# One guard-row tile for two stages, and Toeplitz blocks fetched beside the sample heads

## Chip, cores and metric

The kernel runs on one core of one Trainium2 chip. The metric is the device time of one execution in microseconds (us). Three executions of the kernel before took 2793.55, 2795.27 and 2795.65 us; the median is 2795.27 us.

## What is computed

One layer of a hybrid streaming trunk, in float32, for 2048 prompt frames and 64 frames of a running stream with a 2048-frame cache:

```python
def _layer(x, lp, past):
    h = _rms(x, lp['ln1'])
    q, k, v, fg, u, hc, gb, gc = jnp.split(h @ lp['w_in'], SPLITS, axis=-1)
    ...                                            # q, k normed per head; logf = log_sigmoid(fg + bf)
    att = _fox_prompt(q, k, v, logf)               # 8 heads of 64; or _fox_sample with the caches
    y_ssm, hr, hi = _s5(u, ...)                    # diagonal state space, 16 groups of 16 channels, 64 states
    g = jax.nn.gelu(y_ssm)
    ssm = g * jax.nn.sigmoid(g @ lp['w_glu'] + lp['b_glu'])
    conv, conv_state = _short_conv(hc, gb, gc, lp['conv_w'], conv_prev)
    x = x + concat([_rms(att), _rms(ssm), _rms(conv)]) @ lp['w_out']
    f = jax.nn.relu(_rms(x, lp['ln2']) @ lp['w_up'])
    return x + (f * f) @ lp['w_down'], ...
```

In the attention, a score is `q.k/8 + c_q - c_k`, with c the running sum of the log forget gates, masked causally. The softmax is taken over all earlier frames.

## The kernel before

The stages run one after another: `phase1` (norm, in-projection, convolution; until about 543 us), the attention over eight heads (until about 1200 us), the out-projection, and the two matrices of the feed-forward part. The change touches the end of `phase1` and the attention.

**Scores and guard rows.** A head's transposed scores are two matmuls into a PSUM tile `st`: L1239 with `kb` (67 rows) against `q1`, L1240 with `ka` against `q2`. Rows 0 to 63 of `q1` are the query's high part, rows 64 and 65 are ones (against the forget-gate sums of `kb`, which come from `nc_d`), and row 66 is the guard: minus the row's maximum score, so that the exponential stays in range. `row_max` (L1131) computes that guard. For each of 16 query tiles it multiplies `q1` with `kb` into tiles `mx` (L1149), reduces each into `pm` on the DVE (L1154), transposes the result (`mxt`), copies it to `mt` (L1163) and sends it out by DMA (L1164).

While head h runs, the maxima of head h+1 are computed a piece at a time (`max_items`), and L1164 writes row 66 of the next `q1` from the SP queue. Head 0 has no head before it. Its maxima are computed inside `phase1` (`head0`, L488), where `q1` does not exist yet. So L1164 sends them from ACT's queue to row 2 of the DRAM tensor `m_d`, whose rows 0 and 1 were filled with ones at the start (L557), and L1207, on ACT's queue too, reads all three rows back into `q1`.

**Loads.** `load(h+1)` (L1200 to L1204) issues on the SP queue, at the first unit of head h, the five transfers of the next head's `kb`, `q1` and `ka`. `load_q2` (L1220, L1221) fetches 512 columns of `q2` in two halves, `load_v` (L1212) the 1 MB of `v`. All tile names are per buffer, and two heads' sets alternate. SP issues its DMAs in program order; an instruction that has to wait holds up all behind it. A scheduler has placed the instructions on their queues; the order of emission is that of the code.

**The filler chain.** Between the attention's units, `fill(w)` draws work from one generator, `chain()`: first most of the S5 branch (`s5_branch`), then the 64 sample queries' attention over the cache for head pairs 0 and 1, then pairs 2 and 3 (`sample_attention`), then the rest of the S5 branch and the preparation of the out-projection (`w_out_tiles`, which loads `wo_u` in four transfers). A `yield y` with y over 0 means that the chain pauses for y on a clock that advances with the units; each step drawn also costs a budget. `side_by_side` runs two such generators each with its own clock.

In `s5_branch`, L921 to L924 fetch the Toeplitz matrix `s5mt` from the DRAM tensor `kp_d`: eight transfers of 256 KB on the SP queue, with a `yield 1` after each. After them POOL computes the state recurrence (L931 to L935), and later sends out the final states (L952, L953). `s5mt` is first used after the sample attention.

Of the kernel before, what the change touches and what calls it, by code (L numbers as in the profile page):

```python
# [9 lines left out]
F32 = mybir.dt.float32  # L10
F32R = mybir.dt.float32r
# [8 lines left out]
NP = 2048  # L20
# [28 lines left out]
def f32(ap):  # L49
    return ap.bitcast(F32)  # L50
# [6 lines left out]
def setup(ctx, tc, I, O):  # L57
    g = Ctx()
    nc = tc.nc
    g.tc, g.nc, g.I, g.O = tc, nc, I, O  # L60
    g.dram = ctx.enter_context(tc.tile_pool(name="dram", bufs=1, space=DRAM))
    g.const = ctx.enter_context(tc.tile_pool(name="const", bufs=1, reuse_waits="tile"))
    dram, const = g.dram, g.const

    g.qk_d = [dram.tile([2, 2, 128, NP], F32, name=f"qk_d{i}") for i in range(4)]
    g.v_d = [dram.tile([2, 128, 16, 2 * HD], F32, name=f"v_d{i}") for i in range(4)]
    g.u_d = dram.tile([NT, CH], F32, name="u_d")
    g.mix_d = dram.tile([D, NT], F32, name="mix_d")
    g.kp_d = dram.tile([16, 16, 368], F32, name="kp_d")
    g.r_d = [dram.tile([H, 512], F32, name=f"r_d{i}") for i in range(4)]  # L70
    g.x2_d = dram.tile([NT, D], F32, name="x2_d")
    g.h_d = dram.tile([D, NT], F32, name="h_d")
    g.f_d = dram.tile([DFF, NT], F32, name="f_d")
    g.m_d = dram.tile([3, NP], F32, name="m_d")
    g.l_d = dram.tile([H, NP], F32, name="l_d")
    g.nc_d = dram.tile([3, H, NP], F32, name="nc_d")
    g.s5_d = dram.tile([128, S5N + 256], F32, name="s5_d")
    g.ncs_d = dram.tile([2, H, PAST + NS], F32, name="ncs_d")

    warm = const.tile([128, 1], F32, name="warm")  # L80
    nc.vector.memset(warm, 1.0)
    nc.scalar.activation(warm, warm, AF.Sqrt)
    g.ones = const.tile([128, 1], F32, name="one")
    nc.vector.memset(g.ones, 1.0)
    g.ident = const.tile([128, 128], F32, name="ident")
    make_identity(nc, g.ident)
    g.identb = const.tile([128, 128], BF16, name="identb")
    nc.vector.tensor_copy(g.identb, g.ident)
    g.maskq = const.tile([128, 256], BF16, name="maskq")
    nc.gpsimd.memset(g.maskq, 0.0)  # L90
    nc.gpsimd.affine_select(out=g.maskq, in_=g.maskq, pattern=[[-1, 256]], compare_op=ALU.is_ge,
                            fill=NEG, base=0, channel_multiplier=1)
    g.maskk = const.tile([128, 256], BF16, name="maskk")
    nc.gpsimd.memset(g.maskk, 0.0)
    nc.gpsimd.affine_select(out=g.maskk, in_=g.maskk, pattern=[[1, 256]], compare_op=ALU.is_ge,
                            fill=NEG, base=-128, channel_multiplier=-1)

    g.qbd = const.tile([128, 4, 128], F32, name="qbd")
    nc.vector.memset(g.qbd, 0.0)
    g.kts = const.tile([128, 4, NS], F32, name="kts")  # L100
    g.vs_d = dram.tile([NS, ATT], F32, name="vs_d")
    return g

# [64 lines left out]
def phase1(ctx, g):  # L168
    tc, nc, I, O = g.tc, g.nc, g.I, g.O
    dram = g.dram  # L170
# [8 lines left out]
    sp = ctx.enter_context(tc.tile_pool(name="p1s", bufs=4, reuse_waits="tile"))  # L179
    ps = ctx.enter_context(tc.tile_pool(name="p1ps", bufs=1, reuse_waits="tile", space=PSUM))  # L180
# [283 lines left out]
    for b in range(3):  # L464
# [4 lines left out]
        for gi in range(2):  # L469
            for ti in range(len(BLOCKS[b][gi][1])):  # L470
# [3 lines left out]
                elif gi == 0:  # L474
                    i = where[b - 1, 1 + ti, 0]
                    at(i - 1, loader_x(b, gi, ti))
                    at(i, prepper(b, gi, ti, i))
                else:
                    i = where[b, 0, 0] + ti - 1
# [8 lines left out]
    def head0():  # L488

        r = slice(0, 64)  # L490
        g.mxb = 2
        kt = xtp.tile([128, 8, 384], F32R, tag="xh0", name="kb_h0").rearrange("p k n -> p (k n)")
        qt = xtp.tile([128, 8, 384], F32R, tag="xl0", name="q1_h0").rearrange("p k n -> p (k n)")
        nc.sync.dma_start(f32(kt)[0:64, :NP], g.qk_d[0][0, 1, r, :])
        nc.sync.dma_start(f32(kt)[64:66, :NP], g.nc_d[0:2, 0, :])
        nc.gpsimd.memset(f32(qt)[64:66, :NP], 1.0)
        nc.sync.dma_start(f32(qt)[0:64, :NP], g.qk_d[0][0, 0, r, :])
        yield
        yield from row_max(g, sp, ps, qt, kt, 0, g.m_d[2:3])

    def s5_start():
        sc = xtp.tile([128, 8, 384], F32, tag="xl0", name="s5p").rearrange("p k n -> p (k n)")
# [5 lines left out]
    for i, (b, ci, gi, ti) in enumerate(work):  # L508
# [26 lines left out]
        if len(tails) > 3:  # L535
            f = tails.pop(0)
# [10 lines left out]
def gate_consts(ctx, g):  # L547
    nc, I = g.nc, g.I
    gp = ctx.enter_context(g.tc.tile_pool(name="gate", bufs=1, reuse_waits="tile"))
    tri = gp.tile([128, 128], F32, name="tri")  # L550
    nc.gpsimd.memset(tri, 1.0)
    nc.gpsimd.affine_select(out=tri, in_=tri, pattern=[[1, 128]], compare_op=ALU.is_ge,
                            fill=0.0, base=0, channel_multiplier=-1)
    ones = gp.tile([128, 128], F32, name="ones")
    nc.gpsimd.memset(ones, 1.0)
    nc.gpsimd.dma_start(g.nc_d[2].rearrange("h (a b) -> (h a) b", b=128), ones)
    nc.gpsimd.dma_start(g.m_d[0:2].rearrange("h (a b) -> (h a) b", b=128), ones[0:32])  # L557
    cl = gp.tile([128, 17, H], F32, name="cl")
    nc.vector.memset(cl[64:128, 16, :], 0.0)
    nc.sync.dma_start(cl[:, 0:16, :], I["cache_logf"][0, 0].rearrange("(t p) h -> p t h", p=128))  # L560
    return gp, tri, ones, cl
# [224 lines left out]
def s5_branch(g, pool, sp):  # L786

    nc, I, O = g.nc, g.I, g.O
# [129 lines left out]
        nc.sync.dma_start(hs[hh, 129, :], I[src][0, 0].rearrange("g p -> p g"))  # L918

    mt = pool.tile([128, G, 256], F32, tag="gm", name="s5mt")  # L920
    for t in range(8):  # L921
        nc.sync.dma_start(mt[16 * t:16 * t + 16],
                          g.kp_d[:, :, 16 * (7 - t):16 * (7 - t) + 256].rearrange("g c n -> c g n"))
        yield 1  # L924
    r1 = sp.tile([128, 16, G], F32, tag="yg", bufs=3, name="s5r1")
    r2 = sp.tile([128, 16, G], F32, tag="yg", bufs=3, name="s5r2")

# [200 lines left out]
        yield 0  # L1128


def row_max(g, sp, ps, q1, kb, h, dst):  # L1131

    nc = g.nc
    pm = sp.tile([128, 16, 4], F32, tag="pm", bufs=1, name=f"pm{h}")
    nc.vector.memset(pm, -3e38)
    for t in range(16):
        left, k0, cuts = t + 1, 0, []
        while left:
            w = min(left, 4)
            if left == 5:  # L1140
                w = 3
            cuts.append((k0, w))
            k0 += w
            left -= w
        for c, (k0, w) in enumerate(cuts):
            p = ps.tile([128, 512], F32, tag="mx", bufs=g.mxb, name=f"mx{h}_{t}_{c}")
            last = c == len(cuts) - 1
            n = max(w * 128, 256)
            nc.tensor.matmul(p[:, :n], q1[0:66, t * 128:t * 128 + 128], kb[0:66, k0 * 128:k0 * 128 + n], start=True,  # L1149
                             stop=not last)  # L1150
            if last:
                m = 256 if t == 0 else 128
                nc.tensor.matmul(p[:, n - m:n], g.identb, g.maskq[:, :m], start=False, stop=True)  # L1153
            nc.vector.tensor_reduce(pm[:, t, c:c + 1], p[:, :n], axis=AX.X, op=ALU.max)  # L1154
            yield
    nm = sp.tile([128, 16], F32, tag="nm", bufs=1, name=f"nm{h}")
    nc.vector.tensor_reduce(nm, pm, axis=AX.X, op=ALU.max, negate=True)
    yield
    yield
    pt = ps.tile([128, 512], F32, tag="mx", bufs=g.mxb, name=f"mxt{h}")  # L1160
    nc.tensor.transpose(pt[:16, :128], nm, g.ident)
    mt = sp.tile([16, 128], F32R, tag="mt", bufs=1, name=f"mt{h}")
    nc.vector.tensor_copy(mt, pt[:16, :128])  # L1163
    (nc.sync if h else nc.scalar).dma_start(f32(dst), f32(mt))  # L1164
    yield


def attention(ctx, g, fill):
# [14 lines left out]
    for i in range(2):  # L1183
# [9 lines left out]
            nc.gpsimd.memset(f32(q1[i])[64:67, :], 1.0)  # L1193
        nc.gpsimd.memset(f32(v3[i])[:, :, 128:130], 1.0)

    def load(h):
        i, hp, e = h % 2, h // 2, h % 2
        r = slice(64 * e, 64 * e + 64)
        qk = g.qk_d[hp]
        nc.sync.dma_start(f32(kb[i])[64:67, :], g.nc_d[:, h, :])  # L1200
        nc.sync.dma_start(f32(kb[i])[0:64, :], qk[0, 1, r, :])
        nc.sync.dma_start(f32(q1[i])[0:64, :], qk[0, 0, r, :])
        nc.sync.dma_start(f32(ka[i])[0:64, :], qk[0, 1, r, :])
        nc.sync.dma_start(f32(ka[i])[64:128, :], qk[1, 1, r, :])  # L1204
        if h == 0:
            load_q2(0, 3)
            nc.scalar.dma_start(f32(q1[i])[64:67, :], g.m_d)  # L1207
            load_v(0)

    def load_v(h):  # L1210
# [11 lines left out]
        q2[h, sb] = t  # L1222

    def max_items(h):
        yield from row_max(g, sp, ps, q1[h % 2], kb[h % 2], h, q1[h % 2][66:67, :])

    po = {}

# [627 lines left out]
def hybrid_step_kernel(ctx, tc, I, O, dbg=None):  # L1856
# [3 lines left out]
    with ExitStack() as c2:  # L1860
# [3 lines left out]
        def chain():  # L1864
            for y in s5_branch(g, fpool, fsp):
                if y < 0:
                    yield from sample_attention(g, fpool, fsp, (0, 1))
                    g.idle = True
                    yield from sample_attention(g, fpool, fsp, (2, 3))
                else:  # L1870
                    yield y

# [95 lines left out]
```

## Time and profile before

| | |
|---|---|
| median of three runs | 2795.27 us (2793.55 to 2795.65) |
| profiled execution, its own time | 2794.95 us |
| its span (first to last instruction) | 2793.2 us |
| granted TensorE clock, mean | 0.979 |
| PE busy | 2699.9 us, 97% of the span |
| DVE, ACT, POOL busy | 60%, 44%, 15% |

The profile's lines give the start and length of an instruction, and in brackets the idle time of its engine before it with what ended it. PE is TensorE, DVE is VectorE, POOL is GpSimd, SP is SyncE; SPq and ACTq are those engines' DMA issues, which do not count as busy. PEclk is the granted clock of TensorE: 1.00 is its higher level of 2.4 GHz, 0.50 its lower level of 1.2 GHz.

### The profile page before, as it was taken

What the parts mean: (1) busy time and instruction counts of PE and PEld (TensorE: products, weight loads), DVE (VectorE), ACT (ScalarE), POOL (GpSimd) and SP (SyncE); (2) the same over time, 40 slices, a digit from 0 to 9 for tenths busy, and PEclk for the clock granted to TensorE, in tenths of its full rate; (3) what the DMA queues carried; (4) which work ended last, traced back from release to release, by engine and by line L of the source; (5) the groups of instructions that cost most, each with busy time, mean ns of one, the idle gap of its engine ahead of it and who ended that gap; (6) DMA issues with size and microseconds to landing.
All of it is one profiled execution on the core that took longest, in us unless ns stands there. A gap on an engine that the chain in (4) does not pass through costs nothing.

```text
span 2793.2 us, 38960 instructions
## 1 busy us (share of the span) xinstructions
PE 2699.9 (97%) x14438; PEld 2341.8 (84%) x14438; DVE 1681.7 (60%) x3375; ACT 1230.3 (44%) x2383; POOL 415.4 (15%) x566
## 2 busy tenths in 40 slices
PE   7999999888899999899989999999999999999999
PEld 7999998755567776688789999999998888888887
DVE  7637468477575576577786686686644344434433
ACT  5424243156577677833265676576641111111110
POOL 2101105123752224432300000000000000000000
PEclk9999999989899999999999999999999999999999
DMA  7636546643644223375545353344354122212123
GB/s 216 186 109 185 165 104 177 111 99 93 108 100 109 72 71 89 116 213 165 177 137 176 131 176 127 133 156 136 128 198 151 51 78 80 78 48 78 49 79 117
DMA packets 358929, 347.13 MB, mean 124 GB/s; under 512 B 43726, under 2 KB 316446, under 8 KB 354734
## 3 DMA queue, kind: packets, MB, share of 16 engines
q1 hardware_dynamic: 356189, 336.87, 41.8%
q0 software_dynamic: 2240, 7.01, 0.8%
q8 instruction: 114, 1.87, 0.3%
q14 instruction: 76, 0.62, 0.1%
q10 hardware_dynamic: 310, 0.75, 0.1%
HBM read 237.05 MB, written 107.46 MB: 123 GB/s over the span
## 4 chain that ended last, share of the span: by engine, by line
PE 85%; DMA 4%; issue 4%; DVE 3%; ACT 2%; POOL 1%; SPq 1%; ACTq 0%; DVEq 0%; POOLq 0%
PE pa L1641 12%; PE pd L107 8%; PE pd L108 8%; PE pd L106 8%; PE pd L1641 6%; PE pb L1641 3%; PE pq L106 3%; PE pq L108 3%; PE pq L107 3%; PE mx L1149 2%; PE po L106 2%; PE st L1239 2%; PE po L107 2%; PE po L108 2%; PE st L1240 2%
## 5 line engine op out<-in xcount | busy, mean ns | idle before, releaser
L1820 DVE TENSOR_TENSOR acc<-acc,pd 128x512 f32<-128x512 f32 x272 | 186.7, 686 | 411.2 <-PE pd L108 406.0
L106 PE MATMUL pd<-dw,fh 128*128 128x512 f32 x1016 | 395.2, 389 | 0.0
L108 PE MATMUL pd<-dw,fl 128*128 128x512 f32 x1016 | 395.2, 389 | 0.0
L107 PE MATMUL pd<-dw,fh 128*128 128x512 f32 x1016 | 395.2, 389 | 0.0
L1789 ACT ACTIVATE fh<-fr 128x512 fp32r<-128x512 f32 x127 | 80.2, 632 | 530.9 <-PE pd L107 520.9
L1252 DVE TENSOR_TENSOR pl<-p,ph 128x512 fp32r<-128x512 f32 (+2 forms) x246 | 171.5, 715 | 110.7 <-ACT ph L1251 104.5
L107 PEld LDWEIGHTS pd<-dw,fh 128*128 128x128 f32 x1016 | 190.7, 188 | 39.7
L108 PEld LDWEIGHTS pd<-dw,fl 128*128 128x128 f32 x1016 | 190.7, 188 | 39.6
L106 PEld LDWEIGHTS pd<-dw,fh 128*128 128x128 f32 x1016 | 190.7, 188 | 39.5
L1154 DVE TENSOR_REDUCE pm<-mx 128x1 f32<-128x512 f32 (+2 forms) x320 | 184.3, 607 | 58.7 <-PE mx L1153 32.3
L1248 ACT ACTIVATE p<-st 128x512 f32<-128x512 f32 (+2 forms) x320 | 164.3, 544 | 89.8 <-PE st L1240 34.2
L1641 PE MATMUL pa<-as,wt 128*128 128x352 f32 x1152 | 201.3, 323 | 0.8 <-ACT sm L1656 0.8
L1641 PEld LDWEIGHTS pa<-as,wt 128*128 128x128 f32 x1152 | 187.3, 188 | 2.0 <-ACT sm L1656 1.3
L106 PE MATMUL pq<-wh,xh 128*128 128x384 f32 (+1 forms) x512 | 179.4, 350 | 5.2 <-ACT xh L233 4.7
L1251 ACT ACTIVATE ph<-p 128x512 fp32r<-128x512 f32 (+2 forms) x320 | 173.8, 581 | 3.9 <-PE po L1262 1.8
L108 PE MATMUL pq<-wh,xl 128*128 128x384 f32 (+1 forms) x512 | 174.5, 341 | 0.5 <-DVE xl L234 0.3
L107 PE MATMUL pq<-wl,xh 128*128 128x384 f32 (+1 forms) x512 | 174.1, 340 | 0.0
L1586 DVE TENSOR_TENSOR wt<-tt,wt 128x512 fp32r<-128x512 f32 x192 | 131.4, 687 | 69.1 <-ACT wt L1585 65.9
L1586 DVE TENSOR_TENSOR w<-wr,w 128x512 fp32r<-128x512 f32 x144 | 99.0, 688 | 87.2 <-ACT w L1585 86.9
L1585 ACT ACTIVATE wt<-tt 128x512 fp32r<-128x512 f32 x192 | 120.4, 627 | 67.2 <-PE pd L1641 66.2
L1240 PE MATMUL st<-q,ka 128*128 128x512 f32 (+2 forms) x320 | 124.4, 393 | 12.0 <-DMA q<-qk_d 12.0
L1149 PE MATMUL mx<-kb,q 66*128 66x512 f32 (+2 forms) x280 | 113.4, 438 | 18.1 <-DVE pm L1154 11.1
(508 smaller groups left out, 6118.6 us busy)
## 6 DMA issues: line engine op xcount, KB each, us to landing
wr<-in_w_up_dram SPq DMA_DIRECT2D x46, 1024.0 KB
f_d<-sm SPq DMA_DIRECT2D x47, 704.0 KB
fr<-f_d SPq DMA_DIRECT2D x128, 256.0 KB
raw<-in_w_in_dram SPq DMA_DIRECT2D x51, 512.0 KB
dr<-in_w_down_dram SPq DMA_DIRECT2D x32, 512.0 KB
qk_d<-stgT SPq DMA_DIRECT2D x16, 768.0 KB
xt<-in_x_prompt_dram SPq DMA_DIRECT2D x16, 512.0 KB
ka<-qk_d SPq DMA_DIRECT2D x16, 512.0 KB
```

What stands on the lines that cost most here:

```text
L106: nc.tensor.matmul(out, lh, rh, start=first, stop=False)
L107: nc.tensor.matmul(out, lh, rl, start=False, stop=False)
L108: nc.tensor.matmul(out, ll, rh, start=False, stop=last)
L1149: nc.tensor.matmul(p[:, :n], q1[0:66, t * 128:t * 128 + 128], kb[0:66, k0 * 128:k0 * 128 + n], start=True, stop=not last)
L1154: nc.vector.tensor_reduce(pm[:, t, c:c + 1], p[:, :n], axis=AX.X, op=ALU.max)
L1240: nc.tensor.matmul(st[:, c0:], ka[i][:, kc], q2[h, sb][:, c0:512], start=False, stop=r < 0)
L1248: nc.scalar.activation(p[:, c0:], st[:, c0:], AF.Exp)
L1251: nc.scalar.activation(ph[:, c0:], p[:, c0:], AF.Copy)
L1252: (nc.gpsimd if g.idle and j else nc.vector).tensor_tensor(pl[:, c0:], p[:, c0:], f32(ph)[:, c0:], op=ALU.subtract)
L1586: ve.tensor_tensor(t[:, 1], x, f32(t)[:, 0], op=ALU.subtract)):
L1641: nc.tensor.matmul(bank, w[:, x, k], a[:, y, k], start=first and k + j == 0, stop=k + j == 5, skip_group_check=not first)
L1820: nc.vector.tensor_tensor(a[:, o], a[:, o], p, op=ALU.add)
```

## The change

- `m_d` is gone, and with it the POOL transfer of ones into it. The copy of the transposed maxima goes to one tile, `g.mt`, allocated at the start and kept through both stages.
- For head 0, `load(0)` sends `g.mt` straight to row 66 of `q1` (ACT's queue), and rows 64 and 65 are filled with ones from `nc_d` (SP's queue). For the other heads `max_items` issues the same transfer on SP.
- The eight Toeplitz transfers move from their place in `s5_branch` into a generator `toeplitz`, each behind a `yield 4`, which runs side by side with the sample attention of pairs 2 and 3.

```diff
@@ setup
-    g.m_d = dram.tile([3, NP], F32, name="m_d")
...
+    g.mt = const.tile([16, 128], F32R, name="mt")
@@ phase1
-        yield from row_max(g, sp, ps, qt, kt, 0, g.m_d[2:3])
+        yield from row_max(g, sp, ps, qt, kt, 0)
...
-    nc.gpsimd.dma_start(g.m_d[0:2].rearrange("h (a b) -> (h a) b", b=128), ones[0:32])
@@ s5_branch
-    for t in range(8):
-        nc.sync.dma_start(mt[16 * t:16 * t + 16],
-                          g.kp_d[:, :, 16 * (7 - t):16 * (7 - t) + 256].rearrange("g c n -> c g n"))
-        yield 1
+
+    def toeplitz():
+        for t in range(8):
+            yield 4
+            nc.sync.dma_start(mt[16 * t:16 * t + 16],
+                              g.kp_d[:, :, 16 * (7 - t):16 * (7 - t) + 256].rearrange("g c n -> c g n"))
+
+    g.toeplitz = toeplitz
@@ row_max
-    mt = sp.tile([16, 128], F32R, tag="mt", bufs=1, name=f"mt{h}")
-    nc.vector.tensor_copy(mt, pt[:16, :128])
-    (nc.sync if h else nc.scalar).dma_start(f32(dst), f32(mt))
-    yield
+    nc.vector.tensor_copy(g.mt, pt[:16, :128])
@@ attention
+    def guard(eng, h):
+        eng.dma_start(f32(q1[h % 2])[66:67, :], f32(g.mt))
...
             load_q2(0, 3)
-            nc.scalar.dma_start(f32(q1[i])[64:67, :], g.m_d)
+            nc.sync.dma_start(f32(q1[i])[64:66, :], g.nc_d[2, 0:2, :])
+            guard(nc.scalar, 0)
             load_v(0)
...
-        yield from row_max(g, sp, ps, q1[h % 2], kb[h % 2], h, q1[h % 2][66:67, :])
+        yield from row_max(g, sp, ps, q1[h % 2], kb[h % 2], h)
+        guard(nc.sync, h)
+        yield
@@ hybrid_step_kernel, chain()
-                    yield from sample_attention(g, fpool, fsp, (2, 3))
+                    yield from side_by_side(sample_attention(g, fpool, fsp, (2, 3)), g.toeplitz())
```

How the order of instructions moves is shown at three places. The lines of the changed code are numbered anew: L1202 becomes L1205, L1212 becomes L1216, L1220 and L1221 become L1224 and L1225, L922 becomes L924, L1164 becomes L1197.

ACT's queue at the end of `phase1`, before (`gcs` is a gate of the convolution, `q` in the last row is `q1` of head 0):

```order
L394 ACTIVATE gcs_6381<-pc_6356 128x256
L1164 DMA m_d<-mt_6444 16x128
L394 ACTIVATE gcs_6472<-pc_6447 128x320
L1207 DMA q_6571<-m_d 3x2048
L1248 ACT_TABLE_LOAD
```

The same place now:

```order
L394 ACTIVATE gcs_6380<-pc_6355 128x256
L394 ACTIVATE gcs_6469<-pc_6444 128x320
L1197 DMA q_6568<-mt 1x16x128
L1254 ACT_TABLE_LOAD
L1254 ACTIVATE p_3_0_6604<-st_3_0_6601 128x512
```

One transfer stands where two stood, and it stands behind the last convolution gate instead of ahead of it. SP's queue at the same time, before (`q_3` is the piece of `q2` that head 0 starts with, `kb_6577` the first transfer of head 1):

```order
L1202 DMA q_6571<-qk_d_60 64x2048
L1203 DMA ka_6572<-qk_d_60 64x2048
L1204 DMA ka_6572<-qk_d_60 64x2048
L1220 DMA q_3_6593<-qk_d_60 64x512
L1221 DMA q_3_6593<-qk_d_60 64x512
L1212 DMA v_6573<-v_d_64 128x16x128
L1200 DMA kb_6577<-nc_d 3x2048
```

And now:

```order
L1205 DMA q_6568<-qk_d_60 64x2048
L1206 DMA ka_6569<-qk_d_60 64x2048
L1207 DMA ka_6569<-qk_d_60 64x2048
L1224 DMA q_3_6590<-qk_d_60 64x512
L1225 DMA q_3_6590<-qk_d_60 64x512
L1210 DMA q_6568<-nc_d 2x2048
L1216 DMA v_6570<-v_d_64 128x16x128
L1203 DMA kb_6574<-nc_d 3x2048
```

One small transfer more stands ahead of `v`; the rest keeps its order. SP's queue around the start of head 2, before (`q_6571<-mt` is the guard of head 2; `kb_6577`, `q_6578` and `ka_6575` are head 3's):

```order
L922 DMA s5mt<-kp_d 16x16x256 x2
L1164 DMA q_6571<-mt_8117 1x16x128
L922 DMA s5mt<-kp_d 16x16x256 x4
L1200 DMA kb_6577<-nc_d 3x2048
L1201 DMA kb_6577<-qk_d_61 64x2048
L1202 DMA q_6578<-qk_d_61 64x2048
L1203 DMA ka_6575<-qk_d_61 64x2048
L1204 DMA ka_6575<-qk_d_61 64x2048
L922 DMA s5mt<-kp_d 16x16x256
```

And now (`sa_y` and `sa_c` are the sample attention's keys and forget-gate sums):

```order
L924 DMA s5mt<-kp_d 16x16x256
L1087 DMA sa_y_8241<-in_cache_k_dram 128x4x128
L1197 DMA q_6568<-mt 1x16x128
L1080 DMA sa_c_8354<-ncs_d 4x1x512
L1087 DMA sa_y_8241<-in_cache_k_dram 128x4x128
L1203 DMA kb_6574<-nc_d 3x2048
L1080 DMA sa_c_8417<-ncs_d 4x1x512
L1087 DMA sa_y_8241<-in_cache_k_dram 128x4x128
L1204 DMA kb_6574<-qk_d_61 64x2048
L1205 DMA q_6575<-qk_d_61 64x2048
L1206 DMA ka_6572<-qk_d_61 64x2048
```

Two of the eight Toeplitz transfers remain ahead of head 3's loads (the other one stands three rows above this piece), and four stand behind them, two further on. In their place the sample attention, which has moved forward, sends its own small loads, three of them among head 3's. On PE the matmuls that read these sample keys stand, now, right after head 2's start:

```order
L1245 MATMUL st_3_0_8432<-q_6568,kb_6567 128x512
L1246 MATMUL st_3_0_8432<-q_3_8310,ka_6569 128x512
L1245 MATMUL st_3_1_8439<-q_6568,kb_6567 128x512
L1246 MATMUL st_3_1_8439<-q_3_8310,ka_6569 128x512
L1094 MATMUL sa_ps_8386<-sa_c_8354,sa_i 128x512
L1245 MATMUL st_3_2_8464<-q_6568,kb_6567 128x512
L1246 MATMUL st_3_2_8464<-q_3_8310,ka_6569 128x512
L1245 MATMUL st_3_3_8471<-q_6568,kb_6567 128x512
L1084 MATMUL sa_pk_8419<-ident,sa_y_8241 128x128 x4
```

where before the scores stood alone:

```order
L1239 MATMUL st_3_0_8218<-q_6571,kb_6570 128x512
L1240 MATMUL st_3_0_8218<-q_3_8120,ka_6572 128x512
L1239 MATMUL st_3_1_8225<-q_6571,kb_6570 128x512
L1240 MATMUL st_3_1_8225<-q_3_8120,ka_6572 128x512
L1239 MATMUL st_3_2_8246<-q_6571,kb_6570 128x512
```

`sa_pk` reads the sample keys, and the next transfer into the same piece of `sa_y` can only start behind it.

## Rows read from the trace of the kernel before

**Rows 1.** Stretches: us, busy by engine, PEclk, DMA share, GB/s.

```profile
545.00:550.00 5.00, 0.00 (x0) 0.00 (x0) 0.07 (x3) 0.00 (x0) 0.38 (x3) 0.52 0.29 7
555.00:560.00 5.00, 3.77 (x9) 2.28 (x10) 1.17 (x2) 4.09 (x7) 0.00 (x0) 0.50 1.04 252
664.60:671.50 6.90, 6.40 (x20) 4.90 (x21) 5.73 (x8) 2.78 (x7) 5.39 (x2) 0.51 0.01 2
720.00:740.00 20.00, 13.32 (x63) 8.82 (x61) 8.27 (x10) 8.43 (x17) 18.83 (x24) 0.91 1.07 140
740.00:760.00 20.00, 18.89 (x65) 11.12 (x65) 11.19 (x20) 11.36 (x24) 17.81 (x39) 0.67 0.65 144
760.00:1050.00 290.00, 288.50 (x1594) 208.55 (x1594) 188.62 (x369) 203.04 (x427) 94.49 (x133) 1.00 0.35 88
1056.00:1071.00 15.00, 14.10 (x41) 8.69 (x42) 14.15 (x26) 9.27 (x19) 1.33 (x1) 0.54 0.35 94
```

**Rows 2.** PE in order of time, 542 to 562 us.

```profile
555.07 1.62 PE L1240 MATMUL st<-q,ka 128*128 128x512 f32 x3 [11.61 <-DMA q<-qk_d]
...
559.81 0.67 PE L1260 MATMUL po<-ph,v 128*65 128x512 f32 x1
```

**Rows 3.** Waits of the SP queue, 480 to 620 us: total, times, longest.

```profile
SPq L1220 <- DMA m_d<-mt: 16.1, 1, 16.1
SPq L1221 <- DMA q<-m_d: 1.6, 1, 1.6
```

**Rows 4.** SP in order of time, 538 to 555 us: start, length, issue.

```profile
539.73 0.44 SPq L1220 DMA_DIRECT2D q<-qk_d  x1
541.83 0.45 SPq L1221 DMA_DIRECT2D q<-qk_d  x1
542.32 0.60 SPq L1212 DMA_DIRECT2D v<-v_d  x1
```

**Rows 5.** ACT in order of time, 532 to 556 us.

```profile
532.80 0.35 ACTq L1164 DMA_DIRECT2D m_d<-mt  x1
535.84 0.44 ACT L394 ACTIVATE gcs<-pc 128x320 f32<-128x320 f32 x1 [8.94 <-PE pc L108]
539.74 0.48 ACTq L1207 DMA_DIRECT2D q<-m_d  x1
```

**Rows 6.** POOL in order of time, and its DMA issues, 500 to 560 us.

```profile
540.08 0.71 POOL L419 DMA_DIRECT2D out_dram<-z  x1 [6.65 <-DVE zs L401]
...
out_dram<-z POOLq DMA_DIRECT2D x2, 1.0 KB, 9.0
```

**Rows 7.** SP in order of time, 715 to 728 us.

```profile
715.87 3.47 SPq L922 DMA_DIRECT2D s5mt<-kp_d  x4
...
719.75 0.50 SPq L1201 DMA_DIRECT2D kb<-qk_d  x1
```

**Rows 8.** Chain of waits, 715 to 750 us: start, length, what.

```profile
718.89 8.69 DMA s5mt<-kp_d
...
727.60 19.29 DMA q<-qk_d
```

**Rows 9.** PE in order of time, 720 to 750 us.

```profile
722.11 0.39 PE L1239 MATMUL st<-q,kb 67*128 67x512 f32 x1
...
738.83 0.55 PE L1149 MATMUL mx<-kb,q 66*128 66x256 f32 x1 [6.26 <-issue]
```

**Rows 10.** DMA issues, 700 to 760 us: count, KB each, us to landing.

```profile
out_dram<-s5hs POOLq DMA_DIRECT2D x2, 4.0 KB, 15.7
```

**Rows 11.** PE in order of time, around 665 and 1057 us.

```profile
665.10 0.58 PE L1149 MATMUL mx<-kb,q 66*128 66x256 f32 x1 [3.23 <-DVE pm L1154]
...
1056.85 0.44 PE L1149 MATMUL mx<-kb,q 66*128 66x384 f32 x1 [1.50 <-DVE pm L1154]
```

**Rows 12.** SP in order of time, 1037 to 1043 us.

```profile
1037.32 1.78 SPq L1372 DMA_DIRECT2D wo_u<-in_w_out_dram  x4
...
1040.15 0.48 SPq L1201 DMA_DIRECT2D kb<-qk_d  x1
```

More of the change, by code (lines that the diff above doesn't have):

```diff
@@ L1128, in sample_attention, with row_max @@
         yield 0
-def row_max(g, sp, ps, q1, kb, h, dst):
+def row_max(g, sp, ps, q1, kb, h):
     nc = g.nc
```

## The prediction

> **What bounds the kernel now.** I read the stretches first, for the granted clock and PE's busy time, then PE in order of time for the gaps, then the queue that each gap waits for. PE is the bound: from 760 to 1050 us it is busy 288.50 of 290 us at full clock [rows 1], so other engines' time is worth something only where PE stands still. Two such places lie inside the attention and touch the change.
>
> Place A is the start of the attention. PE stands still for 11.61 us until 555.07, for the query tile [rows 2], and runs at half clock afterwards: 0.50 from 555 to 560 us [rows 1]. What it waits for is the second half of `q2`, issued on SP at 541.83 [rows 4]. The first half had waited on SP for the guard's way into DRAM (16.1 us, the longest wait of the stretch), the second 1.6 us for the way back [rows 3].
>
> Place B is head 2. PE stands still for 6.26 us until 738.83 [rows 9], before the maxima of head 3, and the clock is 0.91 in the 20 us around it and 0.67 in the next 20 [rows 1]. The profile names no releaser. Head 3's `kb` was issued at 719.75, right behind four Toeplitz transfers [rows 7], and the chain of waits shows a Toeplitz transfer 8.69 us in flight and then a piece of `q2` 19.29 us [rows 8], while the DMA engines are full: share 1.07 at 140 GB/s [rows 1]. I read the gap as `kb` and `q1` being late behind them.
>
> **Part A: the guard rows.** One ACT transfer, one POOL transfer (far earlier) and the DRAM round trip go. One ACT transfer and one SP transfer of two rows come, the latter costing SP some 0.45 us, as the neighbouring issue does [rows 4]. The first half of `q2` is free to go up to 16.1 us earlier [rows 3]. The second half now has to wait for the guard's landing, by the eight-deep rotation of the queue's slots, as before for the read back. The guard transfer stands behind the last convolution gate, which ends at 535.84 + 0.44 = 536.28 [rows 5]. Its flight is bounded by the two old ones: 539.74 to 541.83, 2.1 us, for the read [rows 4, 5], and 532.80 to 539.73, 6.9 us, for the write [rows 4, 5]. So SP goes on between 538.4 and 543.2; I take the middle, 540.8, which is 1.0 us earlier than before.
>
> That would let PE start its scores at once, but not its products with `v`. `v` is issued right behind, at 542.32 before [rows 4], and the first `po` comes at 559.81, 4.74 us after the scores resumed [rows 2]. Between them the DMA engines crawl: 7 GB/s at a share of 0.29 from 545 to 550 us [rows 1]. That follows on POOL's writes of the convolution state, issued at 540.08, where 1 KB needs 9.0 us to land [rows 6]. `v` moves 1.0 - 0.45 = 0.6 us forward, still behind them. I estimate the first `po` at 559.2. The half-clock stretch, which ran from 555 on beside the wait for `v`, then begins at 559.2; the nine matmuls at half clock before 560 took 3.77 us, 1.9 us of it for the clock [rows 1], and up to that much is paid after `po` instead. A = -0.6 + 1.1 = +0.5 us. Its ends: if the second half and `v` both slip in front of POOL's writes, the whole 11.6 and the 1.9 go, -13.5; if the guard takes 6.9 us, +1.4 and +1.9, about +3.3.
>
> The Trainium skill, "DMA: Bandwidth & Descriptors", Specifications, says that transfers below 512 B are not at line rate, since the engine reads, modifies and writes; the 1 KB in 9.0 us [rows 6] agrees. The same page, "Issuing engines are not separate DMA queues", says that transfers of ACT, SP and POOL interleave on the same 16 engines. Both speak against a gain from a shorter guard path while POOL's writes stay where they are; by them A would be zero, by the 11.61 us row alone it would be -13.5.
>
> **Part B: the Toeplitz transfers.** Two of eight stay ahead of head 3's loads, so the four right ahead of `kb` [rows 7] and the one behind go. But the sample attention moves into their place, and two of its fetches of keys wait, on SP, for matmuls that stand behind the first scores of head 2 (T0, 722.11 before [rows 9]). Head 3's large loads are queued behind them. Before, they were issued at T0 - 2.4 [rows 7, 9]; I put them at T0 + 2.5, after some fourteen matmuls at 288.50 / 1594 = 0.18 us [rows 1]. In return the flight shortens by the Toeplitz part: 19.3 - 8.7 = 10.6 us [rows 8]. They land at T0 + 13.1. PE came to the maxima at 738.83 - 6.26 = 732.57, T0 + 10.5 [rows 9]; with six more sample matmuls at 0.18 us, T0 + 11.6. That leaves 1.5 us idle. POOL's writes of the S5 states, 15.7 us to land [rows 10], now fall into this flight, so I take 3.0.
>
> Idle saved: 6.26 - 3.0 = 3.3 us. Clock: 18.89 us busy at 0.67 lost 6.2, and the 1.2 us up to 740 at half lost 0.6, together 6.8 [rows 1, 9]. A gap of 3.23 us [rows 11] was followed by 6.40 us busy at 0.51 [rows 1], 3.1 lost. Clock saved: 3.7. Against it: the later sample pairs have less distance between two reads of their one key buffer. The trace of before shows no such wait; from zero to one 3.23-us gap [rows 11], I take 1.5. B = -3.3 - 3.7 + 1.5 = -5.5 us, from -13.1 (all gone) to +3.2 (nothing saved, one new gap).
>
> The remaining six Toeplitz transfers hold SP for 3.47 / 4 = 0.9 us each [rows 7]; they lie under 290 us in which the DMA share is 0.35 [rows 1], and cost nothing unless they stand ahead of another head's loads, which two of them do in head 3.
>
> **Part C: what comes earlier.** Without the eight pauses the chain runs ahead: its last parts stand some 40,000 matmul columns earlier, about a fifth of a head. In head 6 this moves the four `wo_u` transfers, issued at 1037.32 just ahead of head 7's `kb` at 1040.15 [rows 12], away from it, and the DVE work away from the 1.50 us gap at 1056.85 [rows 11]. That place costs 1.5 + 14.10 x 0.46 = 8.0 us [rows 1, 11]. It may vanish or come again elsewhere; I take a quarter, -2.0. Ends: -8.0, and +6.3 for one new gap like that at 665 us with its clock (3.23 + 3.1 [rows 1, 11]).
>
> Sum: +0.5 - 5.5 - 2.0 = -7.0 us on the profiled execution's 2794.95, which is 2788; it stands 0.3 below the median of the runs, so the same against that.
>
> **Rivals.** First, both places open: -13.5 and -13.1 give 2768, one of them with C about 2780. For it speaks that each removed wait is the one that the trace names; against it that POOL's slow writes stay at A and SP's queue waits for PE at B.
>
> Second, no change: A is bound by `v`, and head 3's loads, issued 4.9 us later than before, lose what the Toeplitz transfers give back; the change does only a part of what it says, since two of eight remain in place. Half of C stays: 2792 to 2797.
>
> Third, slower: SP serves its queue in order, and the sample fetches that wait for PE now stand ahead of and among the loads of heads 3 and 4. If a fetch holds the next head's `kb` until more than T0 + 4, the load lands after PE's arrival by as much as before, B saves nothing, and the sample pairs' own waits open gaps inside the 290 us that are clean now. Two such gaps with their clock cost 12.6 us; with C's -2 the time is 2805, with a part of B kept 2801. For it speaks the order on SP; against it that PE passes those matmuls within a few us of T0.
>
> **Chances.** My forecast, 2783 to 2793: 0.47. Both or one place fully open: 0.12. No change: 0.24. Slower: 0.17. What a measurement tells from no change is 0.2%, 5.6 us, so faster is below 2789.7: 0.36 of the forecast and all of the first rival, 0.48. Within: 0.11 and the second rival, 0.35. Slower: 0.17. The range takes most of the third rival and the nearer part of the first: 2777 to 2801.
>
> **What would show it.** A: SP's first half of `q2` as early as 539.73 - 16.1 = 523.6, its second near 540.8; PE's first scores without a wait and then a gap before `po` at about 559; if `po` comes before 553, the first rival holds there. B: the four Toeplitz issues ahead of head 3's `kb` gone, `kb` issued some 2.5 us after head 2's first score, a gap of about 3 us before the maxima of head 3, the clock over 0.8 in the 20 us after it. C: 760 to 1050 us without new gaps, and the half clock after 1057 shorter. The forecast is wrong if the maxima of head 3 still wait over 5 us, or if the sample keys (`sa_pk`) make PE wait.

## The result and the profile after

The changed kernel takes 2812.61 us (median of four runs, 2811.74 to 2814.09) against 2794.96 us for the kernel before. The ratio is 1.0064, with a 95% interval of 1.0047 to 1.0082: it is slower, by 18 us, where 7 us faster were forecast.

Head 2 is where the time goes. Its first score stands at 724.70 us (before 722.11, [rows 9]) and that of head 3 at 830.62 (before 806.94): 105.9 us instead of 84.8. Head 3 loses another 7 us, and some 8 us come back from head 7 on (+27.2 us at its start, +19.0 at the last matmul): PE is idle in it for 3.8 us instead of 8.0, though no sample work stands there in either kernel. Two stretches of the kernel before, heads 2 and 3 (us, busy by engine, PEclk, DMA share, GB/s):

```profile
722.10:806.90 84.80, 77.01 (x363) 50.55 (x362) 56.75 (x92) 51.26 (x104) 76.75 (x146) 0.90 0.52 101
806.90:885.00 78.10, 77.72 (x424) 54.09 (x423) 48.75 (x90) 56.39 (x115) 12.41 (x12) 1.00 0.41 102
```

And of the changed kernel, the two stretches around its largest gap, heads 2 and 3, and the stretch that was clean before [rows 1]:

```profile
720.00:727.00 7.00, 7.00 (x38) 4.76 (x38) 4.36 (x6) 4.03 (x11) 6.79 (x9) 1.00 0.07 2
727.00:735.00 8.00, 0.69 (x4) 0.25 (x3) 1.56 (x2) 0.97 (x2) 7.41 (x11) 0.71 0.19 37
724.70:830.60 105.90, 86.78 (x395) 56.06 (x394) 57.21 (x98) 56.63 (x112) 70.44 (x142) 0.85 0.44 94
830.60:915.70 85.10, 82.08 (x407) 54.55 (x405) 45.64 (x82) 53.12 (x109) 17.10 (x15) 0.94 0.42 101
760.00:1050.00 290.00, 275.97 (x1463) 198.25 (x1463) 172.01 (x339) 186.29 (x391) 87.00 (x117) 0.95 0.36 83
```

In head 2 PE is idle for 105.9 - 86.8 = 19.1 us (before 84.8 - 77.0 = 7.8), at a lower clock. From 727 to 735 us it does next to nothing, and the DMA engines do little either: share 0.19, 37 GB/s. What PE waits for, in order of time (start, length, in brackets the idle time before and what ended it); the first two lines are the start of the attention, the last is head 2:

```profile
548.92 0.77 PE L1245 MATMUL st<-q,kb 67*128 67x512 f32 x1 [5.54 <-DMA q<-nc_d]
...
557.64 0.66 PE L1266 MATMUL po<-ph,v 128*65 128x512 f32 x1 [2.38 <-DMA v<-v_d]
...
734.84 1.11 PE L1084 MATMUL sa_pk<-ident,sa_y 128*128 128x128 f32 x4 [7.31 <-DMA sa_y<-in_cache_k_dram]
```

The waits of PE in head 2, in total, times, longest:

```profile
PE sa_pk L1084 <- DMA sa_y<-in_cache_k_dram: 13.8, 2, 7.3
PE mx L1152 <- DVE pm L1157: 3.4, 6, 0.8
PE sa_pp L1109 <- ACT sa_s L1101: 1.8, 1, 1.8
```

Two fetches of 256 KB of sample keys make 13.8 of the 19.1 us. The chain of waits shows how long each was under way:

```profile
723.43 11.36 DMA sa_y<-in_cache_k_dram
...
779.28 10.17 DMA sa_y<-in_cache_k_dram
```

Beside each of them POOL writes final S5 states, as before [rows 10]: two writes of 4 KB, issued within 3 us ahead of each fetch. POOL in order of time, and the landing of the first two writes:

```profile
721.59 0.90 POOL L955 DMA_DIRECT2D out_dram<-s5hs  x1
...
723.35 0.85 POOL L956 DMA_DIRECT2D out_dram<-s5hs  x1
...
776.28 0.85 POOL L955 DMA_DIRECT2D out_dram<-s5hs  x1
777.78 0.84 POOL L956 DMA_DIRECT2D out_dram<-s5hs  x1
...
out_dram<-s5hs POOLq DMA_DIRECT2D x2, 4.0 KB, 11.9
```

SP's queue, in order of time, at the start of the attention and in head 2:

```profile
526.36 0.45 SPq L1224 DMA_DIRECT2D q<-qk_d  x1
540.93 0.45 SPq L1225 DMA_DIRECT2D q<-qk_d  x1
541.42 0.44 SPq L1210 DMA_DIRECT2D q<-nc_d  x1
541.90 0.56 SPq L1216 DMA_DIRECT2D v<-v_d  x1
...
723.43 0.40 SPq L1087 DMA_DIRECT2D sa_y<-in_cache_k_dram  x1
...
735.98 0.38 SPq L1087 DMA_DIRECT2D sa_y<-in_cache_k_dram  x1
736.42 0.51 SPq L1204 DMA_DIRECT2D kb<-qk_d  x1
```

Head 3's `kb`, issued at 719.75 before [rows 7], leaves at 736.42, right behind the fetch that waited for the late keys.

### The profile page after: what moved, and what is told of

Its sections match the earlier page's. It is cut to its first block, busy times and chain, and to the rows that moved or that the text cites. A ratio compares the mean times of both kernels' runs of the same rounds, so it can differ in the third digit from the quotient of the medians.

```text
span 2812.1 us, 38940 instructions
## 1 busy us (share of the span) xinstructions
PE 2709.6 (96%) x14438; PEld 2345.0 (83%) x14438; DVE 1687.3 (60%) x3370; ACT 1228.6 (44%) x2383; POOL 419.0 (15%) x570
## 4 chain that ended last, share of the span: by engine, by line
PE 84%; DVE 5%; issue 4%; DMA 3%; ACT 3%; POOL 1%; SPq 1%; ACTq 0%; DVEq 0%; POOLq 0%
PE pa L1647 13%; PE pd L107 8%; PE pd L108 8%; PE pd L106 8%; PE pd L1647 6%; PE pb L1647 3%; PE pq L108 3%; PE pq L106 3%; PE pq L107 3%; PE mx L1152 2%; PE po L106 2%; PE po L107 2%; PE po L108 2%; PE st L1245 2%; PE st L1246 2%
## 5 line engine op out<-in xcount | busy, mean ns | idle before, releaser
L1245 PE MATMUL st<-q,kb 67*128 67x512 f32 (+2 forms) x320 | 131.2, 411 | 7.8 <-DMA q<-nc_d 5.5
L1258 POOL TENSOR_TENSOR pl<-p,ph 128x512 fp32r<-128x512 f32 (+1 forms) x79 | 95.1, 1206 | 273.0 <-ACT ph L1257 210.0
```

The lines of the kernel that those rows point to most:

```text
L1245: nc.tensor.matmul(st[:, c0:], kb[i][:, kc], q1[i][:, q0 + c0:q0 + 512], start=True, stop=False)
L1258: (nc.gpsimd if g.idle and j else nc.vector).tensor_tensor(pl[:, c0:], p[:, c0:], f32(ph)[:, c0:], op=ALU.subtract)
```

## The experiments

**The parts apart.** The guard rows alone:

```diff
     (the changed kernel, but in s5_branch the Toeplitz loop as before)
+    for t in range(8):
+        nc.sync.dma_start(mt[16 * t:16 * t + 16], ...)
+        yield 1
-                    yield from side_by_side(sample_attention(..., (2, 3)), g.toeplitz())
+                    yield from sample_attention(..., (2, 3))
```

> Only the guard rows are changed; the Toeplitz transfers and their pauses stand as before. Theory (the loss sits in the sample attention that moved forward into head 2): head 1 starts within 2 us of before and the time is 2793 to 2797 us. Rival 1 (the guard path costs time in all heads, since its transfer now waits on one shared tile): 2800 us or more, spread over the heads.

Measured: 2794.39 us, ratio 0.9994 (0.9983 to 1.0004). Head 1 starts within 0.3 us of before. The loss is not in the guard rows.

The pauses kept, the Toeplitz transfers still moved:

```diff
     (the changed kernel, in s5_branch behind def toeplitz)
+    for t in range(8):
+        yield 1
```

> The changed kernel with the eight pauses of one unit put back where the Toeplitz transfers stood, so that the sample attention starts when it did before, while the Toeplitz transfers still go out beside the later sample heads. Theory: the 21 us lost in head 2 vanish, and the gap before head 3's maxima (6.26 us before the change) shrinks, 2783 to 2792 us. Rival 2 (the moved Toeplitz transfers themselves collide with the sample attention's fetches): 2805 us or more, with the loss in heads 3 and 4.

Measured: 2800.54 us, 1.0019 (1.0009 to 1.0029). The 21 us of head 2 are gone, but the time did not fall below before. Neither side's number held: the pauses decide about 12 us of the loss, and some 5 us remain with the moved Toeplitz transfers. Head 3 is now the longer one, 86.6 us instead of 78.1.

The pauses taken away, the Toeplitz transfers in their old place:

```diff
     (the kernel before)
         nc.sync.dma_start(mt[16 * t:16 * t + 16], ...)
-        yield 1
```

> The kernel before, without the pauses behind the Toeplitz transfers: these go out in one burst where they stood, and the sample attention moves forward as in the changed kernel. Theory: the forward move alone costs what the change costs, 2808 to 2820 us, with PE waiting for sample keys in head 2. Rival 2: without moved Toeplitz transfers no loss, 2793 to 2798 us.

Measured: 2803.42 us, 1.0031 (1.0017 to 1.0045), between the two. PE does wait for sample keys, 3 us ahead of head 2's first score (735.42), and the chain of waits shows that fetch 20 us under way:

```profile
732.53 1.12 PE L1080 MATMUL sa_pk<-ident,sa_y 128*128 128x128 f32 x4 [9.35 <-DMA sa_y<-in_cache_k_dram]
...
712.15 20.34 DMA sa_y<-in_cache_k_dram
```

So the sample attention's move forward, made by the eight pauses that went, opens a gap for keys here too. It is not the changed kernel's gap: this fetch stands right behind the burst of eight Toeplitz transfers, and the run does not divide its 20 us between these and the state writes (720.70 and 722.46).

**The state writes.** First the states as rows, written behind the sample attention:

```diff
-        po.dma_start(O[o][0, 0].rearrange("g p -> p g"), hs[lo, j, :])
-        po.dma_start(O[o + 1][0, 0].rearrange("g p -> p g"), hs[hi, j, :])
+        p = psum(f"s5st{j}")
+        nc.tensor.transpose(p[:16, :128], hs[:, j, :], g.ident)
+        hr = sp.tile([16, 128], F32, tag="ct" if j == 128 else "svn", bufs=1, name=f"s5hr{j}")
+        ac.activation(hr, p[:16, :128], AF.Copy)
+        po.dma_start(O[o][0, 0], hr[:, 0:64])
+        po.dma_start(O[o + 1][0, 0], hr[:, 64:128])
```

> The changed kernel, with the final S5 states transposed on PE and written as rows of 256 B behind the sample attention, in place of writes of single 4-byte elements in head 2 (723 and 777 us). Theory: the element writes held up the sample keys (a fetch of 256 KB in flight for 11.4 and 10.2 us); without them the two gaps of 7.31 and 6.53 us before the sample keys' transposes shrink under 3 us each and the time falls to 2795 to 2803 us. Rival 3 (the fetches are late by SP's order and the single key buffer, whatever POOL writes): gaps within 1.5 us of these, 2809 to 2815 us.

Measured: 2792.84 us, 0.9992 (0.998 to 1.0003), 20 us under the changed kernel and just below the expected range. No wait of PE for sample keys is left in heads 2 and 3; the largest waits there:

```profile
PE mx L1156 <- DVE pm L1161: 3.4, 6, 0.8
PE sa_pp L1113 <- ACT sa_s L1105: 2.5, 2, 1.8
```

That run changed the form of the writes and their place together. Two more separate them. The place alone, still single elements (a copy by ACT, whose buffer is free only behind the sample attention, is written instead of `hs`):

```diff
+        hr = sp.tile([128, 16], F32, tag="ct" if j == 128 else "svn", bufs=1, name=f"s5hr{j}")
+        ac.activation(hr, hs[:, j, :], AF.Copy)
+        po.dma_start(O[o][0, 0].rearrange("g p -> p g"), hr[lo])
     (the imaginary half alike; the two writes from hs go)
```

> The changed kernel, with the S5 states still written as single elements, but from a copy that is only made behind the sample attention, so that the writes go out in heads 5 to 6 instead of head 2. Theory (it is the meeting of element writes and sample keys that costs): the gaps of 7.3 and 6.5 us in head 2 go as with rows, and the time is 2790 to 2800 us, with at most one new gap where the writes now go out. Rival (rows against elements does not matter, a run of other luck): 2808 us or more.

Measured: 2801.44 us, 1.0022 (1.0012 to 1.0031). Both gaps of head 2 are gone. The time is just above the expected range, since head 4 gives back about 10 us around the place to which the writes have moved (92.8 us, against 83.1 in the changed kernel). The gap there, of PE; what ACT, for which PE waits, has waited for itself; and how long that transfer was under way:

```profile
937.47 0.58 PE L1247 MATMUL st<-q,kb 67*128 67x256 f32 x1 [4.07 <-ACT p L1256]
...
936.72 0.22 ACT L956 ACTIVATE s5hr<-s5hs 128x16 f32<-128x16 f32 x1 [7.67 <-DMA mix_d<-sa_ot]
...
926.25 10.38 DMA mix_d<-sa_ot
```

The second copy needs a buffer that the store `mix_d<-sa_ot` reads. That store of 16 KB left SP behind the first element writes (924.83 and 925.72), was under way for 10.38 us, and held ACT's queue, and with it the exponentials for which PE waits. So the writes cost time at the new place as well, by way of another transfer beside them.

The form alone, at the same place. The order of instructions is the same on SP and PE; only the runs differ, 64 B in place of 4 B:

```diff
-        po.dma_start(O[o][0, 0].rearrange("g p -> p g"), hs[lo, j, :])
+        po.dma_start(O[o][0, 0].rearrange("g p -> (g p)").rearrange("(p g) -> p g", g=16), hs[lo, j, :])
     (the imaginary half alike)
```

> The changed kernel with the final S5 states written at the same place, from the same queue and with the same bytes, but with the two axes of the output in the other order (states by groups), so that each partition writes one run of 64 B instead of 16 single elements. No instruction moves on any engine. This run's final states therefore lie in another layout than the reference's. Theory (the single elements hold up the transfers beside them): the gaps of 7.31 and 6.53 us before the sample keys' transposes shrink under 2 us, 2790 to 2800 us. Rival (any write from POOL's queue at that place does it, whatever its runs): gaps as before, 2808 to 2816 us.

Measured: 2793.23 us, 0.9984 (0.9971 to 0.9997). The landing of the writes, head 2 from its first score to that of head 3, the largest waits of PE from 700 to 900 us, and the fetch of keys with the matmuls that read them:

```profile
out_dram<-s5hs POOLq DMA_DIRECT2D x2, 4.0 KB, 1.7
```

```profile
722.96:810.41 87.45, 81.57 (x395) 53.21 (x394) 57.98 (x98) 56.20 (x112) 73.47 (x141) 0.94 0.50 114
```

```profile
PE mx L1152 <- DVE pm L1157: 3.4, 6, 0.8
PE sa_pp L1109 <- ACT sa_s L1101: 2.5, 2, 1.8
```

```profile
721.74 0.39 SPq L1087 DMA_DIRECT2D sa_y<-in_cache_k_dram  x1
...
725.62 0.60 PE L1084 MATMUL sa_pk<-ident,sa_y 128*128 128x128 f32 x4
```

The same 4 KB land in 1.7 us instead of 11.9, and the waits for keys are gone: PE reads the keys, without a wait, 3.9 us after their fetch was issued. Since the work of PE is the same (395 matmuls in head 2), the difference to the changed kernel is the price of the element writes in head 2: 105.9 - 87.5 = 18.4 us, of which 19.1 - 5.9 = 13.2 are idle time and 86.8 - 81.6 = 5.2 the lower clock. This settles the cause of the loss in head 2. Head 3 still takes 83.0 us, against 78.1 in the kernel before; that part is not the state writes' doing.

**What the writes did to the kernel before.** The S5 states as rows (the diff of the first of these runs, on the kernel before):

> The kernel before, with only the final S5 states written as rows of 256 B. Theory (the element writes hold up whatever transfer is in flight, here head 3's loads, which were 19 us on the way): the gap of 6.26 us before head 3's maxima shrinks below 3 us, 2783 to 2792 us. Rival (the Toeplitz transfers ahead of those loads are what makes them late): the gap stays within 1.5 us, 2793 to 2797 us.

Measured: 2790.03 us, 0.9981 (0.9972 to 0.9991), and on PE:

```profile
734.54 0.36 PE L1153 MATMUL mx<-kb,q 66*128 66x256 f32 x1 [1.89 <-issue]
...
743.19 0.77 PE L1244 MATMUL st<-q,ka 128*128 128x512 f32 x1 [1.79 <-DMA q<-qk_d]
```

The gap of 6.26 us [rows 9] is 1.89 with all eight Toeplitz transfers in place: about two thirds of it were the state writes, not the Toeplitz transfers. Head 2 gains less, 3.4 us (81.4 instead of 84.8), as a wait of 1.79 us for `q2` follows. Here form and place changed together.

The convolution states as rows, with the changed guard rows and then with the old ones:

```diff
-            nc.gpsimd.dma_start(O[7][0, 0, :, cs].rearrange("j c -> c j"), z[:, npr:npr + 2])
+            pt = ps.tile([128, 2, 128], F32, tag="t", bufs=2, name=f"zt{half}7")
+            nc.tensor.transpose(pt[:2, 0, :], z[:, npr:npr + 2], g.ident)
+            zr = tp.tile([2, 128], F32, tag="qn", bufs=4, name=f"zr{half}7")
+            nc.vector.tensor_copy(zr, pt[:2, 0, :])
+            nc.gpsimd.dma_start(O[7][0, 0, :, cs], zr)
     (the same for the sample's state, O[13] from zs)
```

> Guard rows changed, Toeplitz transfers as before, and the four last convolution states written as rows of 512 B (a transpose on PE each) in place of single elements. Theory (element writes hold up v at the start of the attention): the gaps at the start of the attention, 6.15 + 0.66 + 2.23 us with the guard rows alone, shrink to under 4 us in all, 2783 to 2791 us. Rival (v is late by its own 1 MB and the place in the queue): the gaps stay over 7 us, 2793 to 2797 us.

Measured: 2779.54 us, 0.9943 (0.9928 to 0.9958), faster than the range. Of the gaps at the start one is left, and the DMA engines move 210 GB/s where the kernel before had 7 [rows 1]:

```profile
547.56 0.50 PE L1249 MATMUL st<-q,kb 67*128 67x512 f32 x1 [1.07 <-ACT p L1258]
```

```profile
548.00:553.00 5.00, 5.00 (x23) 2.82 (x22) 3.73 (x6) 5.00 (x11) 0.51 (x3) 1.00 1.04 210
```

These rows go out at 546.73, some 6 us later than the elements did (540.08, [rows 6]), behind `v`; form and place are not separated at this spot.

> The kernel before, with only the four last convolution states written as rows. If the element writes alone made the start late, the time is that of the run with the guard rows changed as well, 2777 to 2783 us. Theory (the DRAM round trip of the guard is a second wait of its own, which shows once the first is gone): part of the 11.6 us gap remains, 3 to 8 us, and the time is 2782 to 2790 us.

Measured: 2780.97 us, 0.9947 (0.9932 to 0.9962): the first expectation, not the theory's. SP still waits for the DRAM round trip, 10.9 and 3.4 us, and it costs PE half a microsecond:

```profile
546.83 0.50 PE L1247 MATMUL st<-q,kb 67*128 67x512 f32 x1 [1.55 <-ACT p L1256]
```

**All together.** Both kinds of states as rows, with the whole change, with the change and the pauses, and with the guard rows alone:

> The changed kernel with both kinds of states written as rows. Theory: the gain of the start adds to that of head 2, 2778 to 2788 us. Rival: nothing beyond the run with the S5 states alone, 2790 to 2796 us.

> The changed kernel with the eight pauses put back and both kinds of states written as rows. Theory: with element writes gone, both the moved Toeplitz transfers and the guard rows give their gain, 2772 to 2784 us. Rival (the earlier start of the sample attention pays at the end, where head 7 has less filler): slower than the run without the pauses, 2785 us or more.

> Guard rows changed, both kinds of states written as rows, Toeplitz transfers in their old place. Theory (moving the Toeplitz transfers is worth nothing or less, since what made head 3's loads late was the writing of the states): 2772 to 2778 us, faster than the same with the Toeplitz transfers moved (2781 to 2783 us). Rival: 2780 us or more, the Toeplitz move is worth its gap.

Measured: 2781.18 us, 0.9951 (0.9935 to 0.9968); 2782.96 us, 0.9956 (0.9942 to 0.9971); and 2774.77 us, 0.9926 (0.9909 to 0.9942). The last is the fastest version, and beats both kernels. The second is inside its range, but its theory does not hold: the moved Toeplitz transfers give no gain. Moving them costs 6 to 8 us even without the element writes. With the pauses, head 2 does gain by it (706.45 to 783.85, which is 77.4 us from first score to first score, against 82.1 in the last version), but head 3 takes 87.2 instead of 78.2. A row of the second run in head 3:

```profile
800.00:816.00 16.00, 13.19 (x43) 7.74 (x43) 7.88 (x13) 8.19 (x18) 0.00 (x0) 0.68 0.31 91
```

Here PE waits for the maxima of the next head (six gaps behind DVE between 798 and 806 us, 3.4 us in all) and falls to the lower clock, as the kernel before does not in head 3. The same six gaps stand in head 2 of the changed kernel, in the second line of its waits above. Why they come with that order of work was not tried.

## Why the prediction was wrong

**What bounds the kernel.** Right: the time moved only where PE stood still or ran at the lower clock.

**Part A** was put at +0.5 us and is -0.8 at the start of head 1; alone it cannot be told from nothing. The steps held: SP's second half of `q2` left at 540.93 (540.8 forecast, the middle of a range of 4.8 us, so that the hit is in part luck), `v` at 541.90, the first `po` came at 557.64 (559.2 forecast), waiting for `v`. One step was missed: the two rows of ones, costed only by SP's 0.45 us, are now what the first score waits for, 5.54 us. It did no harm, since `v` came later still. That the convolution's element writes hold this place is borne out, as far as the two runs with rows go: both gain 15 us.

The Trainium skill's "DMA: Bandwidth & Descriptors", Specifications, gives 512 B as the least transfer for line rate. What was measured here is another thing, the delay of the transfers beside: the 4-byte runs took 11.9 us and made PE wait for a fetch beside them, while 64-byte runs of the same bytes landed in 1.7 us and no wait for keys was left, though they too are far below 512 B. The same page of the Trainium skill, "Issuing engines are not separate DMA queues", says that transfers run on the same 16 DMA engines, whichever engine started them. The trace agrees: POOL's writes held up SP's fetches.

**Part B** is the step that failed, put at -5.5 us. Three terms of it:

- The reading that `kb` was late behind the Toeplitz transfers. It was mostly late behind the state writes: without these (they were moved and written as rows) 6.26 - 1.89 = 4.4 us of the gap are gone, with the Toeplitz transfers untouched.
- "POOL's writes of the S5 states ... now fall into this flight, so I take 3.0." The writes were seen, but set against the wrong transfer. In that window it was no longer head 3's loads but a fetch of sample keys that was in flight, and PE needs it 4 us after its issue (it stands still from 727.53, the fetch left at 723.43), where it came to head 3's `kb` 12.8 us after the issue before (719.75 to 732.57, [rows 7, 9]). The forecast idle time of 3 us before the maxima did not come (head 3's `kb` left at T0 + 11.7 instead of T0 + 2.5, and was in time all the same); 7.31 us came before the keys' transposes.
- "from zero to one 3.23-us gap ..., I take 1.5" for the sample pairs. Two gaps of 13.8 us together came, and with the clock the element writes cost 18.4 us in head 2.

The moved Toeplitz transfers were to "cost nothing unless they stand ahead of another head's loads"; two of them were seen to stand there, and no time was put on it. With the pauses kept the move costs 5 us, for a reason that is open.

**Part C** was put at -2. Its place was left cleaner: head 6 takes 76.0 us instead of 77.8, at a clock of 0.98 instead of 0.91. But the stretch from 760 to 1050 us, which the forecast called clean, is busy 275.97 us at a clock of 0.95 instead of 288.50 at 1.00; the second gap for sample keys now falls into it. Some 8 us more came back from head 7 on, which no part of the forecast had; what made them was not tried.

Of the rivals the third was right in kind: sample fetches on SP, PE waiting for them, two gaps with their clock. Its price, 12.6 us, was taken from gaps of 3.23 us, and its cause, SP's order, was only half of it: with that order unchanged and the runs 64 B long, 18.4 us of head 2's loss of 21.1 are gone.

## What to carry to other kernels

Look for the transfers that land late for their size (4 KB in 15.7 us, [rows 10]) before costing any move beside them: what is in flight beside them can be late as well, on another queue too. A transfer that is moved away may be worth less than it seems, when it only stood near the cause; and work that is pulled forward brings its own waits into the window of the old one, where a fetch with one buffer has none of the slack that a next head's load had. Write single-element columns as rows, or at least as runs of 64 B.

## What the runs showed of the hardware

Writes of 4 KB in 4-byte elements took 11 to 16 us to land in the windows shown, and two 256 KB fetches of another queue beside them were 10 to 11 us under way; in the first of the two gaps the DMA engines showed a share of 0.19. In runs of 64 B the writes took 1.7 us, and the first of these fetches was there within 3.9 us. A busy share that is low thus does not mean that a transfer beside is free to move.
